# A bidirectional RWKV-7 recurrence on one core: merging two grams, and two head corrections, into one TensorE operation each

## The chip, the cores and the metric

One NeuronCore of a Trainium2 chip runs one layer pair of an encoder trunk in a single launch. The metric is device microseconds of the whole launch; the median of three runs is taken, and each kernel also leaves one profiled execution. TensorE (PE in the rows) multiplies matrices into PSUM, VectorE (DVE) and ScalarE (ACT) read PSUM and write SBUF, GpSimd (POOL) works on SBUF alone, and SyncE (SP) starts the DMAs. All arithmetic of the part that is changed is fp32; one fp32 matmul stands as two records in the trace, so an operation of 8 matmuls reads "x16".

## The reference

The trunk has two layers, each a token mixer and a gated feed-forward block: layer 0 mixes by a Hyena long convolution, layer 1 by RWKV-7 in both directions. SEQ is 512 tokens, D_MODEL 1024, 16 heads of 64. The recurrence that the change touches is, per head, with a 64 x 64 state:

```
def step(state, inp):
    r_t, w_t, k_t, v_t, kk_t, a_t = inp
    sa = einsum('bhvk,bhk->bhv', state, kk_t)
    state = state * w_t - sa * (kk_t * a_t) + v_t * k_t
    return state, einsum('bhvk,bhk->bhv', state, r_t)
y = scan(step, r, w_f, k, v, kk, a) + flip(scan(step, flip(r), flip(w_b), ...))
```

## The kernel before

Layer 1 first makes r, k, v and the low-rank parts for all channels (up to about 915 us of the span, with the value projection running a little longer). Then it walks over 8 tiles of 128 channels; a tile is two heads, h0 on partitions 0 to 63 and h1 on 64 to 127, and holds all 512 tokens as 8 chunks of 64. In place of 512 steps it builds for each chunk and direction d a few 64 x 64 products, inverts a triangular matrix, and carries the state over 8 chunks.

For each tile and direction the work is this. `plan_prep` (L1501 on) makes the decays and the scaled operands r1, r2 and B1. `gram1` (L1585) multiplies them into N and X1, four operations of 64 x 64 x 192. `gram2` (L1609) makes X2 and G: for each half of the chunks (c = 0 and 4) one operation of 8 matmuls for X2, where head hh stays on its own half of the partitions, and one of 8 matmuls for G, where the two heads change halves. Each operation fills one PSUM bank of the tag "pp" (two banks). ACT copies G out of it (512 columns), DVE masks and ACT copies X2 (256 columns each, or in halves of the partitions where d = 1). POOL inverts N (31 steps of two instructions, L1653 and L1655), with DRAM round trips on the way in (Nd) and out (Xi). `plan_operator` merges the inverse's blocks (L1723, L1730), and for each half of the chunks solves (L1750, 8 matmuls into a "po" bank), copies the result to hm on ACT, and corrects: for each head one operation of 4 matmuls (L1767) of 64 rows by 128 columns into one more bank of "po", from which DVE subtracts into P with three instructions (L1771: 512, 256 and 256 columns on 64 partitions). "po" has two banks. `plan_chain` runs the 8 chunks one after another (L1801 on PE, L1806 on ACT, L1809 on DVE), and `plan_finish` normalises and adds the output projection (L1880) to the residual.

The order of the instructions on each engine is fixed when the kernel is built. A planner (`Plan.issue`) holds every operation of all tiles with an engine, a cost in microseconds, its dependencies and its buffers, and emits them one by one, always the one that could start first by its own clock, and among those within one grain the one of the largest remaining path, shifted by hand-set offsets for each section and tile (RW_OFFSET, RW_PLACE). An operation is open only when each of its buffers without a tile has a free slot. So operations of neighbouring tiles are interleaved: gram1 and gram2 of the next tile stand between solve and correction of this one. Ahead of a PE operation the planner can put filler matmuls (L1405, on a tile "busy"), where it expects a gap on PE or where the columns that PE streamed lately fall under a limit (FILL_HARD); they keep PE occupied and compute nothing.

Slots: X2 and G have two each, taken in turn by the two directions; P0 and P1 two each; "pp" and "po" two PSUM banks each; "mm" two; the chain holds the last two of the eight.

Of the kernel before, what the change touches and what calls it, by code (L numbers as in the profile page):

```python
# [9 lines left out]
F32 = mybir.dt.float32  # L10
# [371 lines left out]
}  # L382
RW_MARGIN = 0.026, 0.646
DENSE = 241.3, 6788
FILL_HARD, FILL_LOW, FILL_HIGH, FILL_GAP = 3289, 3274, 3000, 0.25


def pe(n, cols, f=4):
    return n * max(0.165 if f == 4 else 0.06, cols * f / 2400)


def pe64(n, cols):
    return n * (0.026 + cols * 0.00084)
# [6 lines left out]
def act(n, scalars=0):  # L400
    return max(0.2, 0.04 + 0.00093 * n) + 0.093 * scalars


def dve(n, scalars=0):
    return 0.07 + n / 960 + 0.06 * scalars
# [6 lines left out]
class Trunk:  # L412
# [1088 lines left out]
    def plan_prep(self, i, d, T, W):  # L1501
# [3 lines left out]
        nc, p, C0 = self.nc, W["plan"], math.exp(-0.5)  # L1505
        rk, (lhi, llo, olw) = T["rk"], T["lw"]
        h0, h1 = slice(0, 64), slice(64, 128)
# [8 lines left out]
        def tt(o, a, b, op=OP.mult):  # L1516
            nc.vector.tensor_tensor(o, a, b, op)

        def copy(o, a):
            nc.scalar.activation(o, a, AF.Copy)  # L1520

        ps = p.buf("pp", 2, lambda: W["pw"].tile([128, S], F32, name="pp", bufs=2))
        sg = p.buf(f"sg{d}", 1, lambda: W["sg"][d])
        hs = slice(64 * d, 64 * d + 64)
        xw = W["lora"]["w"]
        o = p.op("PE", pe(3, 512, 1), lambda: self.mm3(ps.t, lhi.t[hs, :], llo.t[hs, :], xw[0][hs], xw[1][hs], True, True),
                 olw, [lhi, llo, ps], cols=768)
        o = p.op("ACT", 0.57, lambda: nc.scalar.activation(
            sg.t[:, :, 1:65], ps.t.rearrange("p (c t) -> p c t", t=64), AF.Tanh,
            bias=W["dv"][:, 8 * d + i:8 * d + i + 1], scale=0.5), [o, W["init"][0]], [ps, sg], "exp")  # L1530
        o = p.op("DVE", 0.34, lambda: nc.vector.tensor_scalar(sg.t[:, :, 1:65], sg.t[:, :, 1:65], 1.0, 0.5,
                                                              op0=OP.add, op1=OP.mult), [o], [sg])
        L = p.buf("L", 2, lambda: W["pb"].tile([128, 8, 65], F32, name="L", bufs=2))
        Em = p.buf("Em", 2, lambda: W["pb"].tile([128, 8, 65], F32, name="Em", bufs=2))
        o = p.op("DVE", 0.61, lambda: nc.vector.tensor_tensor_scan(
            L.t.rearrange("p c t -> p (c t)"), W["smask"], sg.t.rearrange("p c t -> p (c t)"), 0.0, OP.mult, OP.add),
            [o, W["load"]["smask"]], [sg, L])
# [5 lines left out]
        r1 = p.buf(f"rhs1{d}{n1}", 1, lambda: W["rhs1"][d][n1])  # L1543
        r2 = p.buf(f"rhs2{d}{n2}", 1, lambda: W["rhs2"][d][n2])
# [13 lines left out]
        if d == 0:  # L1558
            b1 = (2, lambda: Em.t[:, :, a0])
            odn = p.op("DVE", D5, lambda: tt(dn(), ch(1), L.t[:, :, a1]), [ep, T["d_rk"]], [rk, L, r1])  # L1560
            oup = p.op("DVE", D5, lambda: tt(up(), ch(3), L.t[:, :, a1]), [ep, T["d_rk"]], [rk, L, r1])
            ona = p.op("DVE", D5, lambda: tt(nat(), ch(0), Em.t[:, :, a1]), [em, T["d_rk"]], [rk, Em, r2])
# [6 lines left out]
        mn, m1, m2, mr = range(4)  # L1569

        def mask(n, q=slice(0, 128)):
            return W["masks"][q, d, n]
# [3 lines left out]
        on, ox1, ox2, og = [], [], [], []  # L1576
# [20 lines left out]
                N.t[32 * hb:32 * hb + 32, :, 32 * (hb % 2):32 * (hb % 2) + 32]), on, [N]) for hb in range(4)]  # L1597
        for c in range(0, 8, 4):
            cs = slice(c, c + 4)
            for dst in (X2, G):  # L1600
                g = p.buf("pp", 2, lambda: W["pw"].tile([128, 4, 128], F32, name="pp", bufs=2))
                second = dst is X2 or d == 0

                def gram2(g=g, c=c, swap=dst is G, second=second):
                    for e in range(c, c + 4):
                        for hh, oh in ((h0, h1), (h1, h0)):
                            l = r1.t[hh, 9 + e, :] if not swap else r1.t[hh, 7 - e, :] if d == 0 else r2.t[hh, e, :]
                            r = r2.t[hh, e:9:8 - e, :] if second else r1.t[hh, 7 - e:9:e + 1, :]
                            nc.tensor.matmul(g.t[oh if swap else hh, e - c, :], l, r, start=True, stop=True)  # L1609
                o = p.op("PE", pe64(8, 128), gram2, [ona, oup if dst is X2 else odn], [r1, r2, g], cols=1024)  # L1610
                if dst is G:
                    og.append(p.op("ACT", act(512), lambda g=g, cs=cs: copy(G.t[:, cs, :], g.t), [o], [g, G]))
                elif d == 0:
                    ox2.append(p.op("DVE", dve(256), lambda g=g, cs=cs: tt(
                        X2.t[:, cs, 0:64], g.t[:, :, 0:64], mask(m2)[:, None, :].to_broadcast([128, 4, 64])), [o], [g, X2]))
                    ox2.append(p.op("ACT", act(256), lambda g=g, cs=cs: copy(X2.t[:, cs, 64:128], g.t[:, :, 64:128]),
                                    [o], [g, X2]))
                else:
                    for hh, ga, to in ((h0, 64, 0), (h1, 0, 64)):
                        ox2.append(p.op("DVE", dve(256), lambda g=g, cs=cs, hh=hh, ga=ga: tt(  # L1620
                            X2.t[hh, cs, ga:ga + 64], g.t[hh, :, 0:64], mask(m2, hh)[:, None, :].to_broadcast([64, 4, 64])),
                            [o], [g, X2]))
                        ox2.append(p.op("ACT", act(256), lambda g=g, cs=cs, hh=hh, to=to: copy(
                            X2.t[hh, cs, to:to + 64], g.t[hh, :, 64:128]), [o], [g, X2]))
        ogm = p.op("POOL", pool(512), lambda: nc.gpsimd.tensor_tensor(
            G.t[:, :, 0:64], G.t[:, :, 0:64], mask(mr)[:, None, :].to_broadcast([128, 8, 64]), OP.mult), og, [G])
        return dict(X1=X1, X2=X2, G=G, Q=r2 if d == 0 else r1, q=nat if d == 0 else dn, wc=wc, N=N,
# [69 lines left out]
    def plan_operator(self, i, d, T, W):  # L1697
# [14 lines left out]
        def gbuf(n):  # L1712
            return p.buf("po", 2, lambda: W["pw"].tile([128, 512 // n, n], F32, name="po", bufs=2))
# [28 lines left out]
        for c in ((0, 4) if d == 0 else (4, 0)):  # L1742
            cs = slice(c, c + 4)
            g = gbuf(128)
            hm = p.buf("hm", 2, lambda: W["pc"].tile([128, 4, 128], F32, name="hm", bufs=2))

            def solve(c=c, g=g):
                for e in range(4):
                    for q in (h0, h1):
                        nc.tensor.matmul(g.t[q, e, :], M.t[q, c + e, :], X1.t[q, c + e, :], start=True, stop=True)  # L1750
            o = p.op("PE", pe64(8, 128), solve, om + s["ox1"], [M, X1, g, hm], cols=1024)
            if d == 0:
                oh = [p.op("ACT", act(512), lambda g=g, hm=hm: nc.scalar.activation(
                    hm.t[h0].rearrange("p c (a b) -> p c a b", a=2)[:, :, ::-1, :],
                    g.t[h0].rearrange("p c (a b) -> p c a b", a=2), AF.Copy), [o], [g, hm]),
                    p.op("ACT", act(512), lambda g=g, hm=hm: nc.scalar.activation(hm.t[h1], g.t[h1], AF.Copy), [o], [g, hm])]
            else:
                oh = [p.op("ACT", act(512), lambda g=g, hm=hm: nc.scalar.activation(hm.t, g.t, AF.Copy), [o], [g, hm])] * 2
            for h, hh in enumerate((h0, h1)):
                ga = gbuf(128)  # L1760

                def corr(c=c, ga=ga, hm=hm, hh=hh):
                    for e in range(4):
                        l, r = hm.t[hh, e, :], X2.t[hh, c + e, :]
                        if d == 1:
                            l, r = r, l
                        nc.tensor.matmul(ga.t[:, e, :], l, r, start=True, stop=True)  # L1767
                o = p.op("PE", pe(4, 128), corr, [oh[h]] + s["ox2"], [hm, X2, ga, P[h]], cols=512)

                def sub(out, a, b):  # L1770
                    nc.vector.tensor_tensor(out, a, b, OP.subtract)  # L1771
                if h == 0:
                    def swap(t):
                        return t.rearrange("p c (a b) -> p c a b", a=2)
                    subs = ((lambda ga=ga, cs=cs: sub(swap(P[0].t)[h0, cs, 1], s["q"]()[h0, cs, :], ga.t[h0, :, 0:64]), 256, s["Q"], s["oq"]),
                            (lambda ga=ga, cs=cs: sub(swap(P[0].t)[h0, cs, 0], W["ident4"][h0], ga.t[h0, :, 64:128]), 256, None, []),
                            (lambda ga=ga, cs=cs: sub(swap(P[0].t)[h1, cs, ::-1, :], swap(G.t)[h1, cs], swap(ga.t)[h1]), 512, G, s["og"]))
                else:
                    subs = ((lambda ga=ga, cs=cs: sub(P[1].t[h1, cs, 0:64], s["q"]()[h1, cs, :], ga.t[h1, :, 0:64]), 256, s["Q"], s["oq"]),
                            (lambda ga=ga, cs=cs: sub(P[1].t[h1, cs, 64:128], W["ident4"][h1], ga.t[h1, :, 64:128]), 256, None, []),  # L1780
                            (lambda ga=ga, cs=cs: sub(P[1].t[h0, cs, :], G.t[h0, cs, :], ga.t[h0]), 512, G, s["og"]))
                for fn, n, b, dep in subs:
                    s["op"][c // 4].append(p.op("DVE", dve(n), fn, [o] + dep, [ga, P[h]] + ([b] if b else [])))
# [220 lines left out]
```

## Time and profile before

| | us |
|---|---|
| median of three runs | 1845.69 (1842.54 to 1851.92) |
| the profiled execution, whole | 1836.17 |
| its span, first to last instruction | 1834.1 |
| PE, DVE, ACT, POOL busy in the span | 1702.7, 1202.5, 779.7, 850.3 |
| mean granted TensorE clock | 0.966 |

The tiles of the recurrence run from about 915 to 1400 us. Busy times of PE are modelled: a record reaches to the end of its results, past the start of the next one, so the step from one operation's start to the next one's start is the time that PE is taken. Idle time is put down to the instruction that ended it.

### The profile page before, as it was taken

To read this page: it belongs to the slowest core of one execution; us is meant where nothing else is said; L and a number is where in the kernel's file an instruction comes from. 1 tells how busy PE (TensorE), PEld (TensorE's weight loads), DVE (VectorE), ACT (ScalarE), POOL (GpSimd) and SP (SyncE) were. 2 spreads that over 40 slices of the span, in tenths; PEclk is the share of its full clock that TensorE was granted. 3 is DMA by queue.
4 is the path that set the end of the run, shared out by engine and by line. 5 is a ranking of instruction groups with operands and counts; after the bars stand their busy time and mean duration, and the time that the engine had idled before them with its cause. 6 is when DMAs were issued, how large, how long until landed. Compare 5 with 4: busy or idle time off the path is not lost.

```text
span 1834.1 us, 30228 instructions
## 1 busy us (share of the span) xinstructions
PE 1702.7 (93%) x11664; PEld 1342.4 (73%) x11664; DVE 1202.5 (66%) x1901; ACT 779.7 (43%) x1459; POOL 850.3 (46%) x1033
## 2 busy tenths in 40 slices
PE   7999899999999998989888999999998799999997
PEld 5778787787777888766666666676676687777887
DVE  7977996466666005888566678888887666666102
ACT  4543333443344224564323445654564444433322
POOL 5224433544444545555411757755751544444542
PEclk9999999999999999989999989999999899999998
DMA  6434313222222333216414222222211222222333
GB/s 199 132 119 137 115 62 129 77 93 92 90 84 89 107 119 110 81 58 217 163 50 144 61 52 57 44 65 66 44 32 40 78 83 92 92 92 80 104 95 98
DMA packets 123276, 171.64 MB, mean 94 GB/s; under 512 B 59291, under 2 KB 82395, under 8 KB 121596
## 3 DMA queue, kind: packets, MB, share of 16 engines
q1 hardware_dynamic: 123132, 169.70, 29.4%
q8 instruction: 92, 1.51, 0.3%
q14 instruction: 52, 0.43, 0.1%
HBM read 146.07 MB, written 23.59 MB: 93 GB/s over the span
## 4 chain that ended last, share of the span: by engine, by line
PE 42%; DVE 34%; ACT 9%; issue 5%; POOL 4%; DMA 4%; SPq 1%; DVEq 0%; ACTq 0%; POOLq 0%
DVE cv L687 8%; PE mm L486 8%; PE mm L487 8%; PE mm L488 8%; DVE cv L688 3%; ACT cv L686 3%; PE po L1767 3%; ACT whi L476 3%; PE mm L1880 2%; DVE al L574 2%; DVE gs L571 2%; PE pp L1585 1%; ACT ah L573 1%; DVE z L597 1%; DVE r L1156 1%
## 5 line engine op out<-in xcount | busy, mean ns | idle before, releaser
L477 POOL TENSOR_TENSOR wlo<-wraw,whi 128x1024 fp32r<-128x1024 f32 (+1 forms) x124 | 291.6, 2352 | 245.1 <-ACT whi L476 241.9
L486 PE MATMUL mm<-xhi,whi 128*128 128x512 f32 x704 | 281.2, 399 | 17.0 <-DVE z L597 17.0
L488 PE MATMUL mm<-xhi,wlo 128*128 128x512 f32 x704 | 277.8, 395 | 0.0
L487 PE MATMUL mm<-xlo,whi 128*128 128x512 f32 x704 | 277.7, 394 | 0.0
L703 POOL TENSOR_TENSOR wlo<-wraw,whi 128x1024 fp32r<-128x1024 f32 (+1 forms) x69 | 168.2, 2441 | 203.7 <-ACT whi L701 193.0
L687 DVE SCALAR_TENSOR_TENSOR cv<-z,vec,cv 128x512 f32<-128x512 f32 x88 | 163.7, 1861 | 117.1 <-ACT cv L686 117.1
L476 ACT ACTIVATE whi<-wraw 128x1024 fp32r<-128x1024 f32 (+1 forms) x124 | 127.4, 1028 | 124.5 <-PE mm L487 114.5
L486 PEld LDWEIGHTS mm<-xhi,whi 128*128 128x128 f32 x704 | 133.4, 189 | 58.0 <-ACT whi L476 25.7
L488 PE MATMUL mm<-ah,wlo 128*128 128x512 f32 (+1 forms) x440 | 154.1, 350 | 4.7 <-POOL wlo L703 4.7
L488 PEld LDWEIGHTS mm<-xhi,wlo 128*128 128x128 f32 x704 | 133.1, 189 | 30.4
L486 PE MATMUL mm<-ah,whi 128*128 128x512 f32 (+1 forms) x440 | 154.1, 350 | 0.9 <-DVE z L597 0.9
L487 PEld LDWEIGHTS mm<-xlo,whi 128*128 128x128 f32 x704 | 133.4, 190 | 29.1 <-DVE xlo L872 0.3
L487 PE MATMUL mm<-al,whi 128*128 128x512 f32 (+1 forms) x440 | 153.6, 349 | 0.0
L1653 POOL TENSOR_TENSOR T<-X,A 128x126 f32<-128x126 f32 (+22 forms) x217 | 101.2, 466 | 25.5 <-DMA A<-Nd 10.8
L701 ACT ACTIVATE whi<-wraw 128x1024 fp32r<-128x1024 f32 (+2 forms) x79 | 80.0, 1015 | 66.2 <-PE mm L487 44.4
L1655 POOL TENSOR_TENSOR X<-X,T 128x126 f32<-128x126 f32 (+22 forms) x217 | 91.9, 423 | 17.0
L573 ACT ACTIVATE ah<-gs 128x512 fp32r<-128x512 f32 x44 | 27.8, 632 | 164.5 <-DVE gs L571 164.5
L488 PEld LDWEIGHTS mm<-ah,wlo 128*128 128x128 f32 x440 | 82.6, 188 | 17.5 <-POOL wlo L703 5.5
L486 PEld LDWEIGHTS mm<-ah,whi 128*128 128x128 f32 x440 | 82.7, 188 | 13.8 <-ACT whi L476 1.7
L487 PEld LDWEIGHTS mm<-al,whi 128*128 128x128 f32 x440 | 82.7, 188 | 12.1
L589 DVE TENSOR_TENSOR xb<-mm,xb 128x512 f32<-128x512 f32 x10 | 6.9, 693 | 128.3 <-PE mm L488 128.3
L686 ACT ACTIVATE cv<-z,vec 128x512 f32<-128x512 f32 x88 | 71.0, 809 | 18.2 <-DVE z L597 18.2
(456 smaller groups left out, 4018.3 us busy)
## 6 DMA issues: line engine op xcount, KB each, us to landing
wraw<-in_w_up SPq DMA_DIRECT2D x88, 512.0 KB, 3.2
wraw<-in_w_down SPq DMA_DIRECT2D x36, 512.0 KB, 3.5
wraw<-in_hy_w_in SPq DMA_DIRECT2D x22, 512.0 KB, 3.3
Rd<-r SPq DMA_DIRECT2D x32, 256.0 KB, 2.1
rkkb<-Rd SPq DMA_DIRECT2D x8, 1024.0 KB, 5.0
wraw<-in_w_down SPq DMA_DIRECT2D x18, 384.0 KB, 3.1
Kd<-ko SPq DMA_DIRECT2D x36, 128.0 KB, 1.7
K<-Kd SPq DMA_DIRECT2D x4, 1152.0 KB, 5.2
```

The source lines that it names most:

```text
L476: nc.scalar.activation(hi, raw, AF.Copy)
L477: lo_engine.tensor_tensor(lo, raw, hi, OP.subtract)
L486: nc.tensor.matmul(out, whi, xhi, start=first, stop=False)
L487: nc.tensor.matmul(out, whi, xlo, start=False, stop=False)
L488: nc.tensor.matmul(out, wlo, xhi, start=False, stop=last)
L686: nc.scalar.activation(c, z[:, 1:S + 1], AF.Identity, bias=bias, scale=self.v(wname, off + stride))
L687: nc.vector.scalar_tensor_tensor(c, z[:, 0:S], self.v(wname, off), c, op0=OP.mult, op1=OP.add)
L688: nc.vector.scalar_tensor_tensor(c, z[:, 2:S + 2], self.v(wname, off + 2 * stride), c, op0=OP.mult, op1=OP.add)
L701: p.do("ACT", act(n), lambda: nc.scalar.activation(view(hi.buf.t), view(src.buf.t), AF.Copy), [src], [hi])
L703: p.do(lo_engine, c, lambda: e.tensor_tensor(view(lo.buf.t), view(src.buf.t), view(hi.buf.t), OP.subtract), [src, hi], [lo])
L1653: e.tensor_tensor(t, X.t[:, 0:m, j:j + 1].to_broadcast([128, m, n]), A.t[:, j + 1:32, j][:, None, :].to_broadcast([128, m, n]), OP.mult)
L1655: e.tensor_tensor(X.t[:, 0:m, j + 1:32], X.t[:, 0:m, j + 1:32], t, OP.subtract)
```

## The change

X2 and G of one half of the chunks come from one PE operation of 16 matmuls in place of two of 8. Per chunk it issues head h0 on its own half, h1 on its own half, h0 onto the other half, h1 onto the other half. X2 still goes to a "pp" bank; G goes to a bank of GRAM_TAG, which is "po". The planner's cost for the new operation is that of one old one (`pe64(8, 128)`, 1024 columns). It depends on all three scaled operands at once, and names X2 and G among its buffers, so that it is open only when their slots are free. In the same way the decay matmul (L1527) now names sg.

The corrections of the two heads come from one PE operation of 8 matmuls, in which the heads alternate, in place of two of 4. It takes both "po" banks at once, and names both P. The six subtractions on DVE are as before, three for each head. The planner's cost is again that of one old operation (`pe(4, 128)`, 512 columns).

```diff
-        o = p.op("PE", pe(3, 512, 1), ..., olw, [lhi, llo, ps], cols=768)
+        o = p.op("PE", pe(3, 512, 1), ..., olw, [lhi, llo, ps, sg], cols=768)
...
-            for dst in (X2, G):
-                g = p.buf("pp", 2, ...)
-                def gram2(g=g, c=c, swap=dst is G, second=second):
-                    for e in range(c, c + 4):
-                        for hh, oh in ((h0, h1), (h1, h0)):
-                            ...
-                            nc.tensor.matmul(g.t[oh if swap else hh, e - c, :], l, r, start=True, stop=True)
-                o = p.op("PE", pe64(8, 128), gram2, [ona, oup if dst is X2 else odn], [r1, r2, g], cols=1024)
+            g = p.buf("pp", 2, ...)
+            gg = p.buf(GRAM_TAG, 2, ...)
+            def gram2(g=g, gg=gg, c=c):
+                for e in range(c, c + 4):
+                    k = e - c
+                    for hh in (h0, h1):
+                        nc.tensor.matmul(g.t[hh, k, :], r1.t[hh, 9 + e, :], r2.t[hh, e:9:8 - e, :], start=True, stop=True)
+                    for hh, oh in ((h0, h1), (h1, h0)):
+                        ...
+                        nc.tensor.matmul(gg.t[oh, k, :], l, r, start=True, stop=True)
+            o = p.op("PE", pe64(8, 128), gram2, [ona, oup, odn], [r1, r2, g, gg, X2, G], cols=1024)
...
-            for h, hh in enumerate((h0, h1)):
-                ga = gbuf(128)
-                def corr(c=c, ga=ga, hm=hm, hh=hh):
-                    for e in range(4):
-                        l, r = hm.t[hh, e, :], X2.t[hh, c + e, :]
...
-                o = p.op("PE", pe(4, 128), corr, [oh[h]] + s["ox2"], [hm, X2, ga, P[h]], cols=512)
+            pair = [gbuf(128), gbuf(128)]
+            def corr(c=c, pair=pair, hm=hm):
+                for e in range(4):
+                    for ga, hh in zip(pair, (h0, h1)):
+                        l, r = hm.t[hh, e, :], X2.t[hh, c + e, :]
...
+            o = p.op("PE", pe(4, 128), corr, oh + s["ox2"], [hm, X2, *pair, *P], cols=512)
+            for h, ga in enumerate(pair):
```

## Rows read from the trace of the kernel before

**Rows 1.** The page's engines over the span: busy us (share), instructions.

```profile
PE 1702.7 (93%) x11664; PEld 1342.4 (73%) x11664; DVE 1202.5 (66%) x1901; ACT 779.7 (43%) x1459; POOL 850.3 (46%) x1033
```

**Rows 2.** The recurrence's middle: window, length, PE, PEld, DVE, ACT, POOL busy, clock, DMA, GB/s.

```profile
1000.00:1400.00 400.00, 377.01 (x4994) 277.50 (x4992) 327.52 (x753) 214.46 (x554) 241.94 (x504) 0.96 0.22 51
```

**Rows 3.** The same stretch, filler matmuls alone: PE, PEld, POOL, clock.

```profile
1000.00:1400.00 400.00, 28.57 (x170) 12.59 (x170) 0.00 (x0) 0.96 0.22 51
```

**Rows 4.** PE's groups from 915 to 1400 us: count, busy, mean ns, idle before.

```profile
L1609 PE MATMUL pp<-rhs,rhs 64*64 64x128 f32 x1024 | 70.4, 282 | 1.1 <-ACT X L1520 0.7 <-ACT sg L1528 0.4
...
L1767 PE MATMUL po<-hm,X 64*128 64x128 f32 x256 | 36.5, 289 | 0.8 <-DVE P L1771 0.8
```

**Rows 5.** PE in order of time: start, length, line, operation, records (three short stretches).

```profile
1204.74 1.09 PE L1609 MATMUL pp<-rhs,rhs 64*64 64x128 f32 x16
1205.76 0.45 PE L1801 MATMUL ch<-SV,P 128*64 128x64 f32 x8
...
1213.14 1.16 PE L1767 MATMUL po<-X,hm 64*128 64x128 f32 x8
1214.23 0.51 PE L1880 MATMUL mm<-yo,olo 128*128 128x512 f32 x1
...
1163.26 1.71 PE L1767 MATMUL po<-X,hm 64*128 64x128 f32 x16
1164.89 0.73 PE L1880 MATMUL mm<-yo,ohi 128*128 128x512 f32 x2
```

**Rows 6.** All engines about 1218 us, gram2 beside the transposes of v.

```profile
1217.64 1.64 ACT L1520 ACTIVATE X<-pp 64x256 f32<-64x256 f32 x4 [3.60 <-PE pp L1609]
...
1217.87 0.13 PEld L1684 LDWEIGHTS mm<-ident,v 64*64 64x64 f32 x1
...
1217.97 0.28 PE L1609 MATMUL pp<-rhs,rhs 64*64 64x128 f32 x2
...
1217.98 0.22 PE L1684 MATMUL mm<-ident,v 64*64 64x64 f32 x1
...
1218.04 0.22 PE L1684 MATMUL mm<-ident,v 64*64 64x64 f32 x1
...
1218.08 0.28 PE L1609 MATMUL pp<-rhs,rhs 64*64 64x128 f32 x2
...
1218.74 0.22 PE L1684 MATMUL mm<-ident,v 64*64 64x64 f32 x1
...
1218.80 0.22 PE L1684 MATMUL mm<-ident,v 64*64 64x64 f32 x1
```

**Rows 7.** The chain that ended last, 1000 to 1400 us, share by line.

```profile
by line: PE po L1767 12.2%; PE mm L1880 9.8%; PE pp L1609 6.3%; POOL T L1653 5.9%; PE ch L1801 5.9%; POOL X L1655 5.3%; PE pp L1585 5.2%; DVE P L1771 4.8%; PE po L1750 4.5%; issue 3.6%; DVE rhs L1517 3.1%; DMA Xi<-X 3.0%; DVE xb L1884 2.2%;
```

**Rows 8.** DVE's groups from 1000 to 1400 us, the subtractions into P.

```profile
L1771 DVE TENSOR_TENSOR P<-G,po 64x512 f32<-64x512 f32 x60 | 41.0, 683 | 16.8 <-PE po L1767 16.0
...
L1771 DVE TENSOR_TENSOR P<-rhs,po 64x256 f32<-64x256 f32 x60 | 25.1, 418 | 0.9
L1771 DVE TENSOR_TENSOR P<-id,po 64x256 f32<-64x256 f32 x60 | 24.9, 414 | 0.4
```

**Rows 9.** POOL's groups in the same stretch, the inversion.

```profile
L1653 POOL TENSOR_TENSOR T<-X,A 128x126 f32<-128x126 f32 (+22 forms) x217 | 101.2, 466 | 25.5 <-DMA A<-Nd 10.8
L1655 POOL TENSOR_TENSOR X<-X,T 128x126 f32<-128x126 f32 (+22 forms) x217 | 91.9, 423 | 17.0
...
L1644 POOL MEMSET X<- 128x512 f32 x6 | 3.2, 529 | 25.4 <-DMA Xi<-X 25.4
```

**Rows 10.** DVE in order of time, first and last subtraction of one chunk half.

```profile
1215.49 0.69 DVE L1771 TENSOR_TENSOR P<-G,po 64x512 f32<-64x512 f32 x1
...
1220.42 0.42 DVE L1771 TENSOR_TENSOR P<-id,po 64x256 f32<-64x256 f32 x1
```

**Rows 11.** ACT's group that empties G's bank, 1000 to 1400 us.

```profile
L1520 ACT ACTIVATE G<-pp 128x512 f32<-128x512 f32 x28 | 16.4, 592 | 13.2 <-PE pp L1609 12.9
```

**Rows 12.** The longest wait of gram results: us in total, times, longest.

```profile
ACT X L1520 <- DVE X L1517: 37.5, 26, 3.8
```

More of the change, by code (lines that the diff above doesn't have):

```diff
@@ L384 @@
 DENSE = 241.3, 6788
+GRAM_TAG = "po"
 FILL_HARD, FILL_LOW, FILL_HIGH, FILL_GAP = 3289, 3274, 3000, 0.25
@@ L1526, in plan_prep @@
         o = p.op("PE", pe(3, 512, 1), lambda: self.mm3(ps.t, lhi.t[hs, :], llo.t[hs, :], xw[0][hs], xw[1][hs], True, True),
-                 olw, [lhi, llo, ps], cols=768)
+                 olw, [lhi, llo, ps, sg], cols=768)
         o = p.op("ACT", 0.57, lambda: nc.scalar.activation(
@@ L1599, in plan_prep @@
             cs = slice(c, c + 4)
-            for dst in (X2, G):
-                g = p.buf("pp", 2, lambda: W["pw"].tile([128, 4, 128], F32, name="pp", bufs=2))
-                second = dst is X2 or d == 0
-                def gram2(g=g, c=c, swap=dst is G, second=second):
-                    for e in range(c, c + 4):
-                        for hh, oh in ((h0, h1), (h1, h0)):
-                            l = r1.t[hh, 9 + e, :] if not swap else r1.t[hh, 7 - e, :] if d == 0 else r2.t[hh, e, :]
-                            r = r2.t[hh, e:9:8 - e, :] if second else r1.t[hh, 7 - e:9:e + 1, :]
-                            nc.tensor.matmul(g.t[oh if swap else hh, e - c, :], l, r, start=True, stop=True)
-                o = p.op("PE", pe64(8, 128), gram2, [ona, oup if dst is X2 else odn], [r1, r2, g], cols=1024)
[L1611 to L1624, printed above, removed]
@@ new lines, in plan_prep @@
+            g = p.buf("pp", 2, lambda: W["pw"].tile([128, 4, 128], F32, name="pp", bufs=2))
+            gg = p.buf(GRAM_TAG, 2, lambda: W["pw"].tile([128, 4, 128], F32, name=GRAM_TAG, bufs=2))
+            def gram2(g=g, gg=gg, c=c):
[4 more added lines that the diff above has]
+                    for hh, oh in ((h0, h1), (h1, h0)):
+                        l = r1.t[hh, 7 - e, :] if d == 0 else r2.t[hh, e, :]
+                        r = r2.t[hh, e:9:8 - e, :] if d == 0 else r1.t[hh, 7 - e:9:e + 1, :]
+                        nc.tensor.matmul(gg.t[oh, k, :], l, r, start=True, stop=True)
@@ new lines, in plan_prep @@
+            o = p.op("PE", pe64(8, 128), gram2, [ona, oup, odn], [r1, r2, g, gg, X2, G], cols=1024)
+            og.append(p.op("ACT", act(512), lambda gg=gg, cs=cs: copy(G.t[:, cs, :], gg.t), [o], [gg, G]))
+            if d == 0:
+                ox2.append(p.op("DVE", dve(256), lambda g=g, cs=cs: tt(
+                    X2.t[:, cs, 0:64], g.t[:, :, 0:64], mask(m2)[:, None, :].to_broadcast([128, 4, 64])), [o], [g, X2]))
+                ox2.append(p.op("ACT", act(256), lambda g=g, cs=cs: copy(X2.t[:, cs, 64:128], g.t[:, :, 64:128]),
+                                [o], [g, X2]))
+            else:
+                for hh, ga, to in ((h0, 64, 0), (h1, 0, 64)):
+                    ox2.append(p.op("DVE", dve(256), lambda g=g, cs=cs, hh=hh, ga=ga: tt(
+                        X2.t[hh, cs, ga:ga + 64], g.t[hh, :, 0:64], mask(m2, hh)[:, None, :].to_broadcast([64, 4, 64])),
+                        [o], [g, X2]))
+                    ox2.append(p.op("ACT", act(256), lambda g=g, cs=cs, hh=hh, to=to: copy(
+                        X2.t[hh, cs, to:to + 64], g.t[hh, :, 64:128]), [o], [g, X2]))
```

## The prediction

> **What bounds the kernel now.** I read the page's busy shares first, then the stages, then PE by group, then the chain of waits, then what stands beside PE. Over the span PE is 93% busy and no other engine is over 66% [rows 1]. That is an average; the change sits in the recurrence, so I take its middle, 1000 to 1400 us: PE is busy for 377.0 of 400 us, DVE 327.5, POOL 241.9, ACT 214.5, at a clock of 0.96 [rows 2]. PE's figure holds 28.6 us of filler [rows 3], so its own work is 348.4 us, 87% of the stretch; DVE's is 82%. The reader is to see two nearly full engines, not one.
>
> How many tiles lie in that stretch: 60 of each subtraction [rows 8], and a tile has 8 (2 directions, 2 chunk halves, 2 heads), so 7.5 tiles, 53.3 us each. Per tile PE has 46.5 us of its own work (348.4/7.5) and DVE 43.7 (327.5/7.5). POOL's inversion, one tile after another, takes (101.2 + 91.9 + 25.5 + 17.0)/7 = 33.7 us with the idle inside it, and about 25.4/6 + 0.5 = 4.7 us waiting for its buffer to be stored and clearing it [rows 9], some 38 us. So a tile can't get shorter than about 44 us whatever PE does, unless DVE's work changes, and it doesn't.
>
> The chain of waits says the same from the other side: the corrections are 12.2% of it and gram2 6.3%, together 74 us of 400 [rows 7], 9.9 us of a tile.
>
> **Gram2: 64 operations become 32.** 1024 records at 16 for an operation [rows 4] are 64. One takes 1.02 us from its start to the next instruction's (1204.74 to 1205.76) [rows 5]. Does the merged one take 1.02 or twice that? The trace has no operation over all four positions, but it has the mix: at 1217.97 gram2 writes X2, both heads on their own halves (ACT copies X2 out of "pp" there), while the transposes of v (L1684 and L1685), which swap the halves, run between its records. Gram2 steps from 1217.97 to 1218.08, 0.11 us, and the transposes from 1217.98 to 1218.04, 0.06 us; alone, later, they step 1218.74 to 1218.80, the same 0.06 [rows 6]. Eight steps of 0.11 plus a start of about 0.15 is the 1.02 of a gram2 that has PE to itself, so neither slows the other. Bounds for the merged operation: 1.02 (all four at once) and 2.04 (no more overlap than two at a time). I take 1.03, since that row is the thing itself with other data. Saved: 65.3 - 33.0 = 32.3 us over 8 tiles.
>
> The Trainium skill, page "TensorE: Matmul & The Clock Gate", "Part 3: Packing small matmuls — row/col tiling", speaks against this: weight loads overlap matmuls in flight only when the row group differs, and in the merged operation two positions share each row group. The trace doesn't bear it out: the load for L1684 at 1217.87 starts with gram2's matmuls in flight on both row halves [rows 6]. By that rule the merged operation would take its upper bound and gram2 would save nothing.
>
> **Corrections: 64 operations become 32.** Two groups of 256 records, one for each direction, at 8 for an operation [rows 4]. One takes 1.09 us (1213.14 to 1214.23). Where the planner put both heads back to back they already overlap in part: 1.63 us for two (1163.26 to 1164.89) [rows 5], five times in the whole recurrence. So before: 64 x 1.09 - 5 x 0.55 = 67.0 us. In such a pair the second head starts only when the first is half through; with the heads alternating both run from the first matmul. Bounds 1.09 and 1.63; I take 1.10, as 0.54 of overlap in the 1.63 shows two heads running side by side at the single one's pace. After: 35.2. Saved: 31.8 us.
>
> **The sum on PE** is 64 us, 8.0 us a tile: PE's own work falls from 46.5 to 38.5 us, under DVE's 43.7. What is late next is DVE, so most of the 64 can't all be seen.
>
> **What the rest of the change adds.** DVE, ACT and POOL do the same instructions with the same tiles; no DMA is added or moved, and neither SP's nor POOL's queue has a new entry; only their order shifts with the planner's. The new waits are on PE. (a) Gram2 waits for r1, r2 and the slots of X2 and G; before, its results could sit in "pp" until the slot came free (ACT's copies of gram results wait 37.5 us in 26 waits on DVE for reasons of this kind [rows 12]). Behind it in PE's queue stand chain steps, gram1 and the output projection, which the planner can put ahead instead. I take nothing; bounds: a gain of a few us from "pp" being held less, a loss of one longest such wait, 3.8 us, a tile, 30 us in all. (b) The same holds for sg in the decay matmul: nothing, inside the same bounds. (c) The correction waits for both "po" banks and for both P; what DVE has to do behind it comes in one piece, 2 x (0.68 + 0.42 + 0.41) = 3.0 us [rows 8] rather than two of 1.5, and a chain step's multiply queued behind it waits up to 1.5 us longer. In exchange the second head is there 1.1 us or more sooner. DVE's idle time on corrections is 16.0 us in the stretch [rows 8]; some of it goes. I take nothing for the balance; bounds -16 and +1.5 us for each of the 32 pairs, 48. (d) G's bank moves from "pp" to "po": 1.03 us of PE and 0.59 us of ACT [rows 11], four times a tile. Hidden while "po" isn't what a tile waits for; if it is, see the rival below.
>
> **How much of the 64 shows.** Two estimates. First, now a tile takes 53.3 us where its fullest engine has 46.5 us of own work, 87%; if the new one also runs at 87% of its fullest engine, DVE's 43.7, a tile takes 50.1, 3.2 less, 26 us over 8. Second, by the chain: half of its 9.9 us a tile goes, 4.9, 39 us over 8. I take 33, between them, 4.1 us a tile. The profiled execution's own 1836.2 (span 1834.1 and 2.1 around it) would become 1803; the median of the runs stands 9.5 us above that execution, and I put the gain on the median: 1845.7 - 33 = 1813.
>
> **Rivals.**
> 1. All of PE's time shows. For it: PE leads at 94% busy with filler, and DVE's idle time mostly ends on PE. Against it: a tile would have to take 45.3 us with DVE at 43.7, 96%. Gain 50 to 64 us: about 1787.
> 2. The gain is lost between engines: DVE at 82% with PE's work ordered around it, and filler takes the place of what was removed (it is put in wherever the planner counts too few streamed columns, and the merged operations count half as many). Then it is 1837 to 1855, no change.
> 3. Gram2's positions don't overlap beyond two. Then the merged operation takes 2.04 us, the planner believes 1.07, and only the corrections' 31.8 us are there to be had; at the forecast's share (33 of 64) that is 16: about 1829. For it: no operation of the trace holds all four positions. Against it: the steps of [rows 6]. This is also the case of the Trainium skill's rule above, and its 0.07 below is what the trace leaves to it.
> 4. Slower: "po" becomes what a tile waits for. It now has to hold both heads at once, and G too. One chunk half then is a solve of gram2's form, 1.02 [rows 5], its copy, one or two of 0.59 [rows 11], say 0.9, the correction 1.10 and six subtractions 3.0: 6.0 us with both banks tied. Four of them, two pairs of merges (each merge taken as a solve and a copy, 1.6) and half of four G's (1.6 each, one of two banks) make 24.0 + 6.4 + 3.2 = 33.6 us a tile if DVE does nothing else in between. It does: now six subtractions spread from 1215.49 to 1220.84, 5.35 us [rows 10], which makes it 43. It decides from the point where the six take 7.9 us, for then the loop is 53.3, the tile of today. At 9 us a tile takes 57.6, 4.3 more, and the time is 1880. For it: DVE gets fuller as PE gets out of the way. Against it: the planner sees both banks and sets other DVE work behind the subtractions.
>
> A fall of the clock belongs to the bounds rather than to the rivals: one more slice of 16 us at half speed in the stretch costs 8 us.
>
> **How the numbers follow.** Forecast, a gain of 15 to 50 us: 0.53 (its own range 1796 to 1831). Rival 1: 0.15. Rival 2: 0.14. Rival 3: 0.07. Rival 4 with the losses under (a) and (c): 0.11. About 0.5%, 9.2 us, is what a measurement of this kernel tells from no change. Faster is the forecast, rival 1 and most of rival 3: 0.74; within 0.5%: 0.15; slower: 0.11. The range leaves out the far end of rival 1 and rival 4: 1785 to 1849.
>
> **What would show it.** Right: gram2 as 32 operations of 32 records at about 1.03 us to the next start, corrections as 32 of 16 records at 1.10; PE's own work between the start and the end of the recurrence 64 us less; the tile's period (time per 8 subtractions of each kind) near 49 us; DVE's busy share there near 89%; the wait of subtractions for corrections under 16 us. Wrong: gram2 steps of 0.22 us (rival 3); filler or PE idle grown by what was saved at an unchanged period (rival 2); corrections or solves that start late with DVE's subtractions named as what they waited for (rival 4); a period of 46 us or less (rival 1). The prediction also fails if the time changes outside the recurrence, where nothing was touched.

## The result, and the profile after

The changed kernel takes 1857.97 us (median of 7 runs, 1854.6 to 1861.42), the kernel before 1842.05 (7 runs): ratio 1.0085, interval 1.006 to 1.0109. The forecast was a gain of 33 us; it is a loss of 16. One run of e3, at 4206 us, belongs to a slower state and is left out of its median below. The profiled execution after has a span of 1855.4 us at a granted clock of 0.966, the same clock as before.

The machine did what the two operations were meant to do. PE after, in order of time (start, length, line, operation, records), the first steps of a merged gram with one of its weight loads (PEld), what follows the gram, and a merged correction:

```profile
1231.72 0.33 PE L1608 MATMUL pp<-rhs,rhs 64*64 64x128 f32 x2
1231.73 0.33 PE L1612 MATMUL po<-rhs,rhs 64*64 64x128 f32 x2
1231.79 0.14 PEld L1612 LDWEIGHTS po<-rhs,rhs 64*64 64x64 f32 x2
1231.88 0.28 PE L1608 MATMUL pp<-rhs,rhs 64*64 64x128 f32 x2
1231.89 0.28 PE L1612 MATMUL po<-rhs,rhs 64*64 64x128 f32 x2
...
1232.75 0.49 PE L487 MATMUL mm<-lorag,lwghi 128*128 128x512 f32 x1
...
1242.79 1.16 PE L1769 MATMUL po<-hm,X 64*128 64x128 f32 x16
1243.88 0.63 PE L1803 MATMUL ch<-SV,P 128*64 128x64 f32 x14
```

X2's pair and G's pair start 0.01 us apart and step together; the whole operation takes 1.03 us (1231.72 to 1232.75), where one of the two old ones took 1.02 [rows 5]. A correction of both heads takes 1.09, as that of one head did. PE by group from 915 to 1420 us (line, operation, count | busy, mean ns | idle before it), to be read against [rows 4]:

```profile
L1608 PE MATMUL pp<-rhs,rhs 64*64 64x128 f32 x512 | 35.6, 278 | 0.2 <-ACT X L1521 0.2
L1612 PE MATMUL po<-rhs,rhs 64*64 64x128 f32 x512 | 35.3, 278 | 1.3 <-DVE P L1773 1.2
L1769 PE MATMUL po<-X,hm 64*128 64x128 f32 x256 | 20.4, 286 | 0.7 <-ACT M L1738 0.4 <-ACT hm L1758 0.2
L1769 PE MATMUL po<-hm,X 64*128 64x128 f32 x256 | 18.9, 285 | 0.0
```

512 + 512 records at 32 for an operation are 32 grams; 512 at 16 are 32 corrections. PE stands idle for 2.2 us in all before them. Now the stage (window, length, then PE, PEld, DVE, ACT, POOL busy, clock, DMA, GB/s), and under it the filler alone (PE, PEld, POOL):

```profile
1000.00:1420.00 420.00, 360.00 (x5242) 261.54 (x5242) 318.32 (x744) 213.62 (x547) 235.40 (x503) 0.96 0.21 50
1000.00:1420.00 420.00, 75.93 (x513) 47.54 (x513) 0.00 (x0) 0.96 0.21 50
```

PE's own work (busy time without the filler) is 284.1 of 420 us, 68%, where it was 348.4 of 400 [rows 2, 3]. Filler rose from 28.6 to 75.9 us. DVE is 76% busy, not the 89% of the prediction. Outside the recurrence little moved: PE is busy for 857.82 us in the first 915 (before: 857.27) and for 380.75 in the last 415 (380.37 in 414).

The subtractions, DVE in the same stretch, and the chain of waits by line (share of the stretch):

```profile
L1773 DVE TENSOR_TENSOR P<-G,po 64x512 f32<-64x512 f32 x60 | 41.0, 684 | 14.5 <-PE po L1769 12.7 <-POOL olo L1874 0.5
```

```profile
by line: DVE P L1773 8.0%; POOL T L1655 5.8%; POOL X L1657 5.5%; issue 4.9%; PE mm L1882 4.9%; PE ch L1803 4.7%; PE po L1769 4.5%; DVE xb L1886 4.1%; PE po L1752 4.1%; PE po L1406 3.5%; PE pp L1586 2.9%; DVE rhs L1518 2.9%; PE ch L1406 2.8%
```

It is now 420 us that hold 60 subtractions, 7.5 tiles, so a tile takes 56.0 us in place of 53.3. Corrections fell from 12.2% of the chain to 4.5%, gram2 left its head altogether [rows 7]; DVE's wait for corrections fell from 16.0 to 12.7 us [rows 8]. PE's two operations and DVE's wait for them got shorter, and the tile got longer; the subtractions' own share of the chain rose from 4.8 to 8.0%. Filler stands on the chain too (PE L1406, twice, 6.3%), put there by the planner for a gap that it expected on PE or for too few streamed columns.

What did move is the POOL inversion, one tile after another (the first tile's runs on DVE, the other seven on POOL). The last instruction of the sixth inversion on POOL and the first of the seventh, which is the last tile's (start, length, line, operation; in brackets the wait before it), before and after:

```profile
1309.33 0.23 POOL L1655 TENSOR_TENSOR X<-X,T 128x16 f32<-128x16 f32 x1
...
1319.65 0.26 POOL L1653 TENSOR_TENSOR T<-X,A 128x31 f32<-128x31 f32 x1 [1.80 <-DMA A<-Nd]
```

```profile
1305.01 0.23 POOL L1657 TENSOR_TENSOR X<-X,T 128x16 f32<-128x16 f32 x1
...
1337.74 0.25 POOL L1655 TENSOR_TENSOR T<-X,A 128x31 f32<-128x31 f32 x1 [2.74 <-DMA A<-Nd]
```

From there to the end of the span it is 514.4 us before and 517.7 after. The 18 us are lost ahead of it: over the six gaps between its seven inversions POOL stands without one for 95 us before and 125 after, while the six inversions ahead of the last take 10 us less in all. The sixth even ends 4 us earlier than before; the last gap alone grows from 10.1 to 32.5 us.

### The profile page after: what moved, and what is told of

Read it like the earlier page. It is cut to its first block, busy times and chain, and to the rows that moved or that the text cites. A ratio compares the mean times of both kernels' runs of the same rounds, so it can differ in the third digit from the quotient of the medians.

```text
span 1855.4 us, 30940 instructions
## 1 busy us (share of the span) xinstructions
PE 1687.3 (91%) x12022; PEld 1328.0 (72%) x12022; DVE 1197.6 (65%) x1901; ACT 784.1 (42%) x1461; POOL 845.2 (46%) x1033
## 4 chain that ended last, share of the span: by engine, by line
PE 39%; DVE 36%; ACT 11%; issue 5%; POOL 5%; DMA 3%; SPq 1%; DVEq 0%; ACTq 0%; POOLq 0%
DVE cv L688 8%; PE mm L487 8%; PE mm L488 8%; PE mm L489 8%; DVE cv L689 3%; ACT cv L687 3%; ACT whi L477 2%; DVE P L1773 2%; DVE al L575 2%; DVE gs L572 2%; ACT ah L574 1%; DVE z L598 1%; PE mm L1882 1%; POOL T L1655 1%; POOL X L1657 1%
## 5 line engine op out<-in xcount | busy, mean ns | idle before, releaser
L1655 POOL TENSOR_TENSOR T<-X,A 128x126 f32<-128x126 f32 (+22 forms) x217 | 96.9, 447 | 38.4 <-DMA A<-Nd 23.8
L1406 PEld LDWEIGHTS <-busy 128*32 128x32 bf16 x716 | 66.8, 100 | 58.4 <-issue 35.8
```

Source lines behind the costliest of these rows:

```text
L1406: nc.tensor.matmul(t, busy[:, 0:32], busy, start=True, stop=True)
L1655: e.tensor_tensor(t, X.t[:, 0:m, j:j + 1].to_broadcast([128, m, n]), A.t[:, j + 1:32, j][:, None, :].to_broadcast([128, m, n]), OP.mult)
```

## The experiments

Theories at the start. T1: the names cost it; an operation open only when both "po" banks, both P, X2 and G are free makes tiles wait (rival 4, the losses under (a) to (c)). T2: PE's time is worth little here, and the planner's new order, whatever drew it, costs the 16 us. Ratios with 95% intervals, each to runs of the kernel before made beside it (their medians lie between 1840.3 and 1842.1):

| kernel | us | ratio | last inversion starts | from there to the end |
|---|---|---|---|---|
| before | 1842.05 | 1 | 1319.7 | 514.4 |
| after | 1857.97 | 1.0085 (1.006 to 1.0109) | 1337.7 | 517.7 |
| e1 G in "pp" | 1856.35 | 1.0068 (1.0042 to 1.0095) | 1336.4 | 518.1 |
| e2 gram merged only | 1840.17 | 1.0012 (0.9987 to 1.0037) | 1322.1 | 515.9 |
| e3 corrections merged only | 1848.63 | 1.0035 (1.0015 to 1.0056) | 1324.2 | 517.9 |
| e4 after, PE time put back | 1864.99 | 1.0128 (1.0108 to 1.0148) | 1342.0 | 519.7 |
| e5 before, names only | 1860.22 | 1.0107 (1.0085 to 1.013) | 1336.6 | 520.8 |
| e6 before, numbers jittered | 1847.05 | 1.0035 (1.0014 to 1.0056) | 1328.5 | 516.3 |
| e7 after, new order | 1828.79 | 0.9938 (0.9919 to 0.9958) | 1312.1 | 510.4 |
| e8 = e2, new order | 1820.24 | 0.9888 (0.9867 to 0.9909) | 1307.8 | 512.7 |
| e9 before, new order | 1845.33 | 1.003 (1.0011 to 1.0049) | 1326.8 | 513.9 |
| e10 = e2, second order | 1839.04 | 0.9991 (0.9972 to 1.001) | 1323.4 | 516.9 |
| e12 = e5, new order | 1838.05 | 0.9989 (0.9977 to 1.0) | 1321.2 | 513.1 |
| e13 = e7, PE time put back | 1834.64 | 0.9965 (0.994 to 0.9989) | 1326.9 | 515.9 |
| e14 = e8, gram's time put back | 1825.39 | 0.9925 (0.9898 to 0.9952) | 1305.5 | 514.3 |
| e15 after, second order | 1826.16 | 0.9938 (0.9915 to 0.9961) | 1327.3 | 511.9 |
| e16 after, third order | 1840.22 | 0.9996 (0.9979 to 1.0014) | 1328.5 | 512.4 |
| e17 = e2, third order | 1828.4 | 0.9929 (0.9901 to 0.9956) | 1309.9 | 514.5 |
| e18 = e2, fourth order | 1818.66 | 0.9889 (0.9867 to 0.9911) | 1305.3 | 509.9 |

The last two columns are from one profiled execution each, which can lie several us from the median (e15's is 15 above it).

**e1: G's bank back in "pp".**

```diff
-GRAM_TAG = "po"
+GRAM_TAG = "pp"
```

> The changed kernel with G's bank taken from pp again (GRAM_TAG = "pp"), all else as changed. If the two po banks are what a tile waits for since G moved there, the time falls under the kernel before's 1842, and the subtractions of a chunk half stay closer together. If the loss lies in the order into which the planner now puts the operations, the tag matters little: 1845 to 1870, with PE filler still near 76 us in the recurrence.

Measured 1.0068, like the change itself. G in "po", rival 4's trigger, isn't the cause.

**e2 and e3: one half of the change each.** e2 is the changed kernel with the corrections of before, e3 the kernel before with the merged corrections.

```diff
e2, against after:
-            pair = [gbuf(128), gbuf(128)]
+            for h, hh in enumerate((h0, h1)):
+                ga = gbuf(128)
...
e3, against before: the same lines the other way round
```

> X2 and G from one operation as in the change, but the corrections as two operations again. If the merged correction (both po banks and both P at once) makes the loss, this one keeps the gram's gain: 1815 to 1840. If naming X2 and G on the gram makes it, it stays at 1850 to 1865. On PE 32 us less of own work than before either way.

> The corrections of both heads from one operation, gram2 as two operations again. If the merged correction makes the loss: 1850 to 1870. If the gram's named buffers or G in po make it: 1815 to 1840.

The gram alone is neutral (1.0012) though by the rows above it takes 32 us off PE; the corrections alone lose some (1.0035). Neither gains; their sum, 0.47%, is below the change's 0.85%, but not by more than the intervals allow.

**e4: the PE time put back, in the changed kernel's own order.** Costs and names as told to the planner are unchanged, so the order is too; only the matmuls inside each operation are sorted so that they overlap less.

```diff
 def gram2(g=g, gg=gg, c=c):
     for e in range(c, c + 4):
         ...  # X2
+    for e in range(c, c + 4):
+        k = e - c
         ...  # G
 def corr(c=c, pair=pair, hm=hm):
-    for e in range(4):
-        for ga, hh in zip(pair, (h0, h1)):
+    for ga, hh in zip(pair, (h0, h1)):
+        for e in range(4):
```

> The changed kernel with the same order of operations on every engine, but inside the merged gram all matmuls of X2 stand before those of G, and inside the merged correction all of head 0 before head 1, so that most of the side-by-side running is lost: by the rows of before some 0.7 us more for a gram and 0.55 us for a correction, 40 us of PE in all. If PE's time is what the changed kernel lacks, it grows by 25 to 40 us, to about 1890. If PE has slack in this order and other waits set the time, it grows by under 12 us: 1855 to 1870, and the filler or PE's idle time shrinks instead.

PE in order of time, a gram and a correction of e4:

```profile
1199.75 1.71 PE L1771 MATMUL po<-hm,X 64*128 64x128 f32 x16
1201.39 0.49 PE L1884 MATMUL mm<-yo,ohi 128*128 128x512 f32 x1
...
1218.04 0.71 PE L1608 MATMUL pp<-rhs,rhs 64*64 64x128 f32 x10
1218.49 0.33 PE L1614 MATMUL po<-rhs,rhs 64*64 64x128 f32 x2
...
1218.87 0.71 PE L1614 MATMUL po<-rhs,rhs 64*64 64x128 f32 x10
1219.51 0.61 PE L1406 MATMUL po<-busy 128*32 128x256 bf16 x4
```

This gram takes 1.47 us, most others of the trace 1.52 (1.03 in the change), and the correction 1.64 (1.09), so 32 x 0.49 + 32 x 0.55 = 33 us were put back, not the 40 expected: G's first records run ahead into X2's tail. The kernel lost 7.0 us by it (1864.99 against 1857.97). So in this order 33 us of PE are worth about 7: this is the first direct price of PE time, about a fifth, where the forecast had taken half. (Its bearing on the clock is below, with e13 and e14.)

**e5: only the names.** The kernel before, nothing merged, with the new names on its operations.

```diff
-                  olw, [lhi, llo, ps], cols=768)
+                  olw, [lhi, llo, ps, sg], cols=768)
-                o = p.op("PE", pe64(8, 128), gram2, [...], [r1, r2, g], cols=1024)
+                o = p.op("PE", pe64(8, 128), gram2, [...], [r1, r2, g, dst], cols=1024)
```

> The kernel before with only the new names among the buffers: sg on the decay matmul, X2 or G on the gram2 operation that fills it; no operation is merged and each G stays in pp. If waiting for the slots of X2 and G on PE is what costs, it is slower by most of what the changed kernel is, 1850 to 1860. If the naming is free it is within 1836 to 1847. If any change of what the planner is told re-orders the recurrence for the worse, it is slower too, though no PE time was taken away: this run alone does not part the first from the last, e6 does.

1.0107: the loss of the whole change, with no operation merged. Its stage and its filler:

```profile
1000.00:1420.00 420.00, 395.56 (x5028) 289.33 (x5026) 323.20 (x747) 213.48 (x549) 237.32 (x504) 0.94 0.21 49
1000.00:1420.00 420.00, 37.56 (x230) 17.89 (x230) 0.00 (x0) 0.94 0.21 49
```

PE's own work is 358.0 us here and 284.1 after, DVE 323.2 and 318.3, and both end about as late. Filler is 37.6 us against 75.9, so the loss doesn't need the added filler; no run took it out. At this point T1 (waits on the named slots) and T2 (the names only redraw the order) were still both alive.

**e6: the order alone.** The kernel before, with each RW_OFFSET of the recurrence moved by a random few units, as

```diff
-("gram1", "PE"): -137.7   ("merge0", "SP"): 92.8   ("operator0", "PE"): -162.9
+("gram1", "PE"): -136.1   ("merge0", "SP"): 90.6   ("operator0", "PE"): -172.4
```

> The kernel before, same operations and buffers, with the recurrence's order numbers in RW_OFFSET moved by random amounts (normal, 10 wide, on numbers from -1071 to 1189; one draw). If the old order was a favourable one among near ones, this is slower by 10 to 40 us though every instruction is the same. If the order of near alternatives is worth little, it stays within 1836 to 1847, and the merged kernel's loss must come from its operations or their buffers.

1.0035: a change that touches no operation costs 0.35%. The numbers of before suit the operations of before better than this one draw near them.

**e7 to e10, e12 and e15 to e18: the numbers fitted anew.** RW_OFFSET and RW_PLACE were found by changing a few at random and keeping what shortened the planner's own end, each time for the kernel in question; e9 is the control (the kernel before, treated likewise). In e9, e10 and e16 the planner was also told a cost of 1.09 or 1.1 for a correction. The numbers of the same three entries:

```diff
-before, after  ("gram1", "PE"): -137.7   ("merge0", "SP"): 92.8    ("operator0", "PE"): -162.9
+e7  (after)    ("gram1", "PE"): -147.7   ("merge0", "SP"): 472.2   ("operator0", "PE"): -884.3
+e15 (after)    ("gram1", "PE"): -134.8   ("merge0", "SP"): -260.8  ("operator0", "PE"): -1295.2
+e16 (after)    ("gram1", "PE"): -142.2   ("merge0", "SP"): 1838.2  ("operator0", "PE"): -1187.6
+e8  (e2)       ("gram1", "PE"): -137.9   ("merge0", "SP"): 267.4   ("operator0", "PE"): -161.9
+e10 (e2)       ("gram1", "PE"): -136.2   ("merge0", "SP"): -30.9   ("operator0", "PE"): -161.0
+e17 (e2)       ("gram1", "PE"): -139.4   ("merge0", "SP"): 170.9   ("operator0", "PE"): -152.8
+e18 (e2)       ("gram1", "PE"): -137.5   ("merge0", "SP"): 117.4   ("operator0", "PE"): -159.0
+e9  (before)   ("gram1", "PE"): -137.7   ("merge0", "SP"): -295.6  ("operator0", "PE"): -156.7
+e12 (e5)       ("gram1", "PE"): -138.3   ("merge0", "SP"): 397.2   ("operator0", "PE"): -173.3
```

> The changed kernel, same operations, names and buffers, with other order numbers in RW_OFFSET and RW_PLACE, found by changing a few at random and keeping what shortened the planner's own end. If the loss is one of order alone, it drops below 1842, and by the gain that the forecast saw it could reach 1815. If the merged operations' buffers (both po banks at once, X2 and G held from the gram on) make the loss whatever the order, it stays at 1850 or more.

> e2 (only the gram merged) with order numbers found in the same way. If order is what hides the gain, it is the better of the two, as the correction still frees its banks one by one: 1805 to 1830. If DVE and the loop through the inversion already set the time of the kernel before, no order gains: 1836 to 1845.

> The control for e7 and e8: the kernel before, unmerged, its order numbers sought in the same way and as long, with the planner told 1.09 us for a correction in place of 0.853, as the trace of before has it. If e7 and e8 gained from the merge and order only repaired what the merge had upset, this one stays within 1832 to 1846. If any kernel gains by new numbers, it falls to about 1820 too and the merge was worth nothing.

> e8 once more with the correction told at 1.09 us and numbers sought for that. If the planner's wrong price of the correction still costs order, it beats e8's 1820 by 3 to 10 us; if not, it is within 5 us of it.

> e5 (before with only the new names, 19 us slower) with order numbers sought in the same way. If naming X2 and G on PE costs by itself, it stays over 1850. If e5's loss was order, it comes back to 1835 to 1846, where before is.

> The changed kernel with a second, independently found set of order numbers, of nearly the planner's end of e7's. If e7's gain is a property of the merged kernel in a fitted order: 1820 to 1838. If e7 was a lucky draw: 1840 or more.

> The changed kernel with the merged correction told at 1.10 us in place of 0.853 and numbers sought for that, a third draw. A fitted order again: 1820 to 1838; if orders scatter on the chip by what the planner doesn't see: anywhere from 1820 to 1855.

> e8's kernel with an independently found set of order numbers. If e8's gain belongs to the kernel in a fitted order: 1815 to 1832. If it was a lucky draw: 1833 to 1850. Either way the time follows the start of the last inversion, 510 to 521 us before the end of the span.

> A fourth independent order of the same kernel, with the same two readings: 1815 to 1832, or 1833 to 1850.

e12 settles T1 for the gram's names: what cost 1.0107 in one order costs nothing in another (0.9989). e7 and e15 are the whole change, all names and both merges, at 0.9938: the change as built loses 16 us, and the same operations in two other orders gain 12 and 14. e9 does not gain (1.003), so the gain isn't what new numbers give to any kernel. But e10 and e16, merged and fitted in the same way, stand at 0.9991 and 0.9996. These two and e9 are just the runs in which the planner was told the correction's longer cost; the five merged kernels fitted at the old cost all gain (0.9888 to 0.9938). So e9 is the control of e10 and e16, and the unmerged kernel fitted at the old cost is e12, at 0.9989 with the new names. At either cost the merged kernels come out ahead of the unmerged one, by 0.3 to 1.0%, with one draw for each control. Why the truer cost gave no better order is open.

e18's stage and filler, in its shorter recurrence, for [rows 2, 3]:

```profile
1000.00:1400.00 400.00, 364.44 (x5149) 264.05 (x5148) 331.78 (x764) 219.10 (x561) 242.52 (x506) 0.98 0.23 54
1000.00:1400.00 400.00, 47.72 (x306) 25.60 (x306) 0.00 (x0) 0.98 0.23 54
```

PE's own work is 316.7 us of 400, DVE's 331.8, 83%: DVE, not PE, is the fuller engine. Its last inversion starts at 1305.3, 14 us before that of the kernel before.

**e13 and e14: is the gain of the new orders PE time?** e7's order with both operations slowed as in e4, and e8's with the gram alone slowed. e11 has a label that says the same, but the kernel that ran under it was e7 unchanged: a second trace of e7, one run of 1828.79 us, the last inversion at 1316.6.

```diff
 e13: the edit of e4, in e7
 e14: the gram2 part of it, in e8
```

> e7 once more, for a second look at its trace: 1824 to 1833, the last inversion starts near 1312 us and filler in the recurrence is near 80 us.

> e7 (both merges, reordered, 1829) with the same order on every engine, but X2 before G inside the gram and head 0 before head 1 inside the correction, some 40 us more on PE in all. If e7's gain is freed PE time, this gives back most of 12 us or more: 1840 to 1870. If PE has slack there too and order alone made the gain, it stays within 8 us: 1829 to 1837.

> e8 (gram merged, reordered, 1820) with the same order, but X2 before G inside the gram, some 23 us more on PE. If e8's gain is freed PE time: 1835 to 1845. If order alone: 1820 to 1827.

e13 loses 5.9 us against e7 for 33 us of PE put back, e14 5.2 against e8 for 16 (32 x 0.49). The intervals of each pair overlap, so these are prices of 5 to 6 us with an uncertainty of about that size; with e4 the three agree. What e14 keeps (it is still at 0.9925) came with the order or with what is left of the overlap.

The clock hides a part of these prices. The mean granted clock over the runs is 0.965 for after, e7 and e8, and 0.969, 0.969 and 0.966 for e4, e13 and e14: PE was granted more clock in the runs with the sorted operations. Over the 20 runs of the kernel before made beside e1 to e4, 0.01 less clock goes with 13 us more time. At an equal clock, by this estimate, e4 would have lost about 12 us, e13 about 11 and e14 about 6: a third or a little more of the PE time put back, not a fifth. The same estimate takes some 5 us off e5's loss (0.960 against 0.964). It explains nothing of the change's loss, for after and before have the same clock (0.965 and 0.964).

## Why the prediction was wrong

- **PE's 64 us: right.** 1.03 and 1.09 us an operation, 32 of each; own work 348.4 in 400 us before and 284.1 in 420 after, 7.5 tiles each. Rival 3 fell. The rule of the Trainium skill ("TensorE: Matmul & The Clock Gate", "Part 3: Packing small matmuls — row/col tiling"), that a weight load overlaps matmuls in flight only in another row group, disagrees with the trace: the load for G at 1231.79 starts with matmuls on both row halves in flight since 1231.72 and 1231.73, and the operation isn't longer for it.
- **"How much of the 64 shows": mis-sized.** I took half, 33 us, because PE led at 94% busy and its operations were 18.5% of the chain. In a fixed order (e4) 33 us of PE are worth 7, or about 12 at an equal clock; so the 64 are worth some 14 to 23, if the second half of them has the price of the first. The likely reason, which no run shows by itself, is that with two engines at 82 to 87% and neighbouring tiles interleaved another path of nearly the same length stands beside PE's; the chain names only what was last in one execution.
- **"Only their order shifts": the step that failed.** The order was priced at nothing, without a reason. It is the largest term, and it turned the sign: with the 64 us worth 14 to 23, a loss of 16 leaves 30 to 39 us for the order that the planner drew (an estimate). Runs that change the order with little else show the size: names alone 19 us (e5), a jitter of the numbers 6 (e6), a fit for the merged operations 29 the other way (e7 against after). The bound under (a), a loss of 30 us, was the right size for the wrong reason: a wait for slots, which e12 and e7 show need not cost anything.
- **Rival 4 fell:** DVE's wait for corrections went down to 12.7 us, e1 moved G's bank and nothing changed, and e7 and e15 tie both "po" banks in the same way and gain. **Rival 2** described the signs (filler took the place, the period didn't fall) but said no change; it has no term for an order that loses.
- **Where the 18 us are.** The time follows the start of the last inversion: over all kernels of the table that start moves from 1305 to 1342, while what comes after it stays within 510 to 521. The traces show a loop that fits. r1 and r2 have two slots in use by turns of the tiles: tile i+2's write into them waits for tile i's last subtraction that reads them, and behind that write stand gram1, its trip through DRAM and the inversion. DVE in order of time at that place, for the last tile, before and after:

```profile
1299.49 0.42 DVE L1771 TENSOR_TENSOR P<-rhs,po 64x256 f32<-64x256 f32 x1
1299.95 2.00 DVE L1517 TENSOR_TENSOR rhs<-rkkb,L 128x512 f32<-128x512 f32 x2
```

```profile
1316.91 0.42 DVE L1773 TENSOR_TENSOR P<-rhs,po 64x256 f32<-64x256 f32 x1
1317.37 1.29 DVE L1518 TENSOR_TENSOR rhs<-rkkb,L 128x512 f32<-128x512 f32 x2
```

In both the write starts 0.46 us after the subtraction starts, and the inversion 20 us after the write (1319.65 and 1337.74); the subtraction itself is 17 us later. Of these 17, 6 were there when POOL had inverted the tile that the subtraction belongs to (its end at 1249.8 before and 1256.1 after); 11 were added between that end and the subtraction. The other traces read the same: in every one of the table the last such write follows a subtraction that reads rhs as DVE's next instruction, 0.46 to 0.53 us behind its start, and the last inversion starts 15 to 21 us after the write, while the subtraction itself moves from 1286.5 (e18) to 1320.8 us (e4). So a correction that an order puts late delays the inversion two tiles on. The loop is read from the traces; a third slot, which would have tested it, wasn't tried, and what puts the corrections late in an order isn't shown.

**Open:** what in an order makes it a good one. e7, e15 and e16 issue the same operations, as do e8, e10, e17 and e18, and their ratios spread over 0.6 and 1.0%. How much of e18's 1.1% belongs to the merge and how much to a lucky order can't be divided beyond the 5 to 6 us that e14 shows; against it stand two controls, e9 and e12, of one draw each.

The best version is e18: the gram merged, the corrections as before, the numbers fitted to it: 1818.66 us, 0.9889 (0.9867 to 0.9911). e8, the same operations, is level with it.

## What to carry to other kernels

A written-out order with fitted numbers is part of the kernel: any new operation, cost or buffer name redraws it, and here that alone was worth from -1% to +1%. So price the edit in a fixed order first (make the operation slow again without telling the planner, as e4 does), and compare kernels only after the numbers are fitted to each, with a control that is fitted at the same costs. A busy share with filler in it is no bound, and half of a freed engine's time is no default: here it was a fifth, or a third at an equal clock. So compare the granted clock of the two runs as well.

## What the runs showed of the hardware that was not expected

Sorting the matmuls of one operation is enough to lose about half of the overlap: with X2 ahead of G, G's first record starts 0.45 us after X2's (e4, 1218.04 and 1218.49), when ten of X2's sixteen records have started, and the operation takes 1.47 to 1.52 us, where full overlap gives 1.03 and none would give 2.04; interleaved, both start within 0.01. For the corrections it is 1.64 us between 1.09 and 2.18. So in these traces a later matmul on other positions starts ahead of earlier ones, but only by a few records, six in the gram of e4.
